# A macaron hybrid block on one Trainium2 core: hidden tiles turned by DMA are joined three weight products after they are parted, and the two newest units of down column 3 come after the seven-product block

## The chip, the cores and the metric

The kernel runs on one core of a Trainium2 chip. The metric is the device time of one execution in microseconds (us). Before the change its median over three runs was 1768.29 us (1766.9 to 1770.48). The engines are written as in the profile: PE is the matrix engine (PEld its weight loads), DVE the vector engine, ACT the scalar engine, SP the engine whose queue issues almost all DMAs.

## The reference

One layer: a half-step SwiGLU FFN, a mixer of two head groups, a second half-step FFN, a final norm. All in float32, 256 tokens, width 2048, FFN width 5632.

```python
def swiglu_ffn(x, w_gate, w_up, w_down):
    return (jax.nn.silu(x @ w_gate) * (x @ w_up)) @ w_down
...
    x = x + FFN_RESIDUAL_SCALE * swiglu_ffn(rms_norm(x, ffn1_norm[l]),
                                            ffn1_w_gate[l], ffn1_w_up[l], ffn1_w_down[l])
    z = rms_norm(x, mix_norm[l]) @ w_in[l]
...
    x = x + y @ w_out[l]
    x = x + FFN_RESIDUAL_SCALE * swiglu_ffn(rms_norm(x, ffn2_norm[l]),
                                            ffn2_w_gate[l], ffn2_w_up[l], ffn2_w_down[l])
return rms_norm(x, final_norm)
```

The change touches the two FFNs, and two small buffers of the norms.

## The kernel before, in words

**Weights.** Every weight comes as a unit of 512 rows by 512 columns (1 MB, tile `raw`). A unit is split into a high part (two ACT casts, `hi`) and the rest (one DVE subtraction, `lo`), and each matrix product is the sum of three matmuls: high by high, high by low, low by high (`parts_of`, line 173, and `multiply`, line 198). One call of `multiply` is one weight product: 12 matmuls of 512 columns for one token tile, 24 for two. There are three sets of `hi`/`lo` buffers in an FFN, three `raw` buffers, and two more (`kept`) that take the first two units of every seven-product block and, in the FFN, two of every five other units.

**FFN.** The FFN width is cut into 11 units of 512. Unit 0 is made first. Then stage s (0 to 4) makes two more units: a seven-product block for the gate (`seven`, line 343, called in line 738), one for up (line 739). A seven-product block is a 2x2 block product (2 token tiles by 2 column units, first two row units) with seven products of 12 matmuls in place of eight, with sums of the weights made by DVE in place (`raw` minus `raw`), and the other row units by the usual products of 24 matmuls: two of them per column unit in gate and up. Its loads are all emitted at its beginning. `done` hands out each of its four results as it is complete: in the up block that is `up` (line 730), which multiplies by the gate's silu and calls `turn_hidden` (line 423). After stages 0, 2 and 4 `down` (line 646) multiplies the finished units (three, four, four of them) by their rows of the down matrix and adds to the residual `xres`.

**Turning a tile.** Down needs the hidden tile with FFN columns on the partitions. `turn_hidden` parts a tile of 128x512 floats into two planes of 16-bit halves (ACT, tile `plane`), lets a DMA on SP's queue transpose it (line 431), joins the halves again (ACT, back into `plane`), splits it into high (ACT) and low (DVE) in `hidden[u]`, and where the tile is the newest of a down, copies it back once more (`turned`, ACT). There is one `plane` buffer, so the next tile can be parted only when the one before is joined and split. Each up block makes four tiles, unit 0 two: 44 tiles in all.

**Down.** Of its units, m and n are the two newest, the others are older. Column 0 and column 3 of the output are plain sums over units (`add_units`, line 660: one load, one split, one product of 24 matmuls per unit); columns 1 and 2 are one seven-product block in which m and n are the 2x2 block and the others the usual products. `block_sums` (line 679) makes the sums of the m and n tiles that the block needs. In stage 0 there is one other unit, in stages 2 and 4 two. The order of the calls stands in `plan` and `tail` (lines 693 to 707):

- stage 0: column 0 of others and n, column 3 of the other and n, column 0 of m, sums, column 3 of m, block;
- stage 2: column 0 of others and n, column 3 of others, column 0 of m, sums, column 3 of n and m, block (in FFN 1 with `prepare`, small vectors of the mixer, ahead of it);
- stage 4: column 0 of others and n, column 3 of others, column 0 of m, sums, block, column 3 of n and m.

**Order.** A tile scheduler puts the instructions of each engine in an order when the program is built; earlier code has precedence, but an instruction that is expected to be ready goes ahead of one that is not. Engines work their queue in that order. Only stretches with `Engine.pinned` keep the order of the code.

Nearly all rows of the profile name line 43, the helper that issues instructions; so they are read by tile names: `ps_g`, `ps_u`, `ps_d` are products of gate, up and down, `_a _c _e _d` the four banks of a seven-product block, `hi_.._p`/`lo_.._p` the split units of its seven products, `_x` those of its usual ones, `hs` the sums of hidden tiles, `u_g`, `z`, `s_g` the tiles that hold hidden tiles, `h` the turned tile's halves.

Of the kernel before, what the change touches and what calls it, by code (L numbers as in the profile page):

```python
# [10 lines left out]
F32 = mybir.dt.float32  # L11
F32R = mybir.dt.float32r
U16 = mybir.dt.uint16
# [4 lines left out]
P = 128  # L18
# [31 lines left out]
def hybrid_block(ctx: ExitStack, tc: tile.TileContext, a: dict, out: bass.AP):  # L50
# [35 lines left out]
    def f32(ap):  # L86
        return ap.bitcast(F32)
# [252 lines left out]
    def quad(tile):  # L340
        return tile.rearrange("p (j c) -> p j c", j=UK)
# [63 lines left out]
    def ffn(tag, norm, after, opening=False):  # L405
        with (
# [8 lines left out]
                return fp.tile([P, CW], dt, tag="keep", name=name, bufs=13)  # L415

            def plane():
                return fp.tile([P, CW], F32, tag="plane", name=f"plane{tag}", bufs=1)

            hidden = {}  # L420
            turned = {}

            def turn_hidden(u, t, h, again):

                if u not in hidden:
                    hidden[u] = big(f"h{tag}_{u}")
                pt = plane()
                mixed = "p (f b) -> p b f"
                flat = "p (b f) -> p b f"
                act.copy(pt.bitcast(U16).rearrange(flat, b=2), h.bitcast(U16).rearrange(mixed, b=2))  # L430
                nc.sync.dma_start(
                    h.bitcast(U16).rearrange("p (r c) -> p r c", c=P), pt.bitcast(U16), transpose=True
                )
                act.copy(pt.bitcast(U16).rearrange(mixed, b=2), h.bitcast(U16).rearrange(flat, b=2))
                pt = pt.rearrange("p (j c) -> p j c", j=UK)
                hi = hidden[u][:, :, t * P : (t + 1) * P]
                lo = hidden[u][:, :, S + t * P : S + (t + 1) * P]
                act.copy(hi, pt)
                dve.tensor_tensor(lo, pt, f32(hi), op=ALU.subtract)
                if again:  # L440
                    act.copy(quad(h), pt)
                    turned[u, t] = quad(h)

            units, vs, sf, ready = [], {}, {}, []

# [198 lines left out]
            turn_of["hold"] = False  # L644

            def down(last):
                us = sorted(hidden)
                others, (m, n) = us[:-2], us[-2:]
                end = last and tag == 2

                def update(c, t, *parts):
                    xr = xres[:, t, c * CW : (c + 1) * CW]
                    for p in parts:
                        dve.scalar_tensor_tensor(xr, p, 0.5, xr, op0=ALU.mult, op1=ALU.add)
                    if last:
                        after(c, t)

                side = {c: [bank(f"ps_d{tag}_{m}_{c}_{t}") for t in range(NT)] for c in (0, 3)}

                def add_units(c, units):  # L660
                    blks = [
                        (u, unit(wd[u * UK * P : (u + 1) * UK * P, c * CW : (c + 1) * CW], f"d{tag}_{m}_{c}_{u}"))
                        for u in units
                    ]
                    groups = [[0], [1]] if end and units == [n, m] else [[0, 1]]
# [12 lines left out]

                def block_sums():
                    seven_of(  # L680
                        sh, hidden[m], hidden[n],
                        {(t, i): turned[u, t] for t in range(NT) for i, u in ((0, m), (1, n))},
                        quad(keep(f"hspare{tag}_{m}")),
                        [[quad(keep(f"hs{tag}_{m}_{i}_{z}", F32R)) for z in range(2)] for i in range(4)],
                    )()

                def add(t, b, ps, tiles):
                    got[t, b] = [ps] + tiles
                    if (0, b) in got and (1, b) in got:
                        for i in range(NT):  # L690
                            update(2 - b, i, *got[i, b])

                plan = [(0, [u]) for u in others + [n]] + [(3, [u]) for u in others]
                if len(others) == 1:
                    plan.append((3, [n]))
                plan.append((0, [m]))
                tail = [(3, [n, m])] if end else [(3, [u]) for u in (n, m) if (3, [u]) not in plan]
                for step in plan:
                    add_units(*step)
                block_sums()  # L700
                if not last:
                    for step in tail:
                        add_units(*step)
                if tag == 1 and m == 5:
                    prepare()
                seven(wd, (m, n), (2 * CW, CW), sh, [(u, hidden[u]) for u in others], f"d{tag}_{m}", keep, add)
                if last:
                    for step in tail:
                        add_units(*step)
                hidden.clear()  # L710
                turned.clear()

            for s in range(5):
# [26 lines left out]
                if s % 2 == 0:  # L740
                    down(s == 4)
            extra.clear()


    def small(name):
# [337 lines left out]
```

## Time and profile before

| | |
|---|---|
| median of 3 runs | 1768.29 us |
| the profiled execution | 1769.3 us |
| its span, first to last instruction | 1767.5 us |
| mean granted PE clock | 0.991 |
| PE, weight loads, DVE, ACT busy | 1721.6, 1419.8, 1486.8, 1137.2 us |
| HBM read | 339.82 MB, 193 GB/s over the span |
| hidden tiles turned (casts of `h` out of `plane`) | 44 |
| transposing DMA, issue to landing | 3.0 to 7.8 us |

Busy time is a union of spans; matmuls overlap, and 20182 instructions are shared out over the engines. A row of the windows gives a stretch, its length, and busy time with the number of instructions of each engine in it; the granted clock is in parts of full speed.

### The profile page before, as it was taken

Reading aid. Unit: us, or ns where it says so; the run is one execution under the profiler, and the core shown is the slowest. Engines: PE = TensorE matmul, PEld = TensorE weight load, DVE = VectorE, ACT = ScalarE, POOL = GpSimd, SP = SyncE. Lnnn points to the kernel's source line nnn. Section 1 sums busy time; section 2 is a strip of 40 time slices with the busy share of each in tenths; the row PEclk is TensorE's granted clock in tenths of the full one; section 3 lists DMA queues with packets and bytes.
Section 4 is the critical chain, followed back from the end, with each engine's and each line's share of the span. In section 5 each row is a group of like instructions: output and inputs, shape, how many; then the busy total and the mean of one; then the engine's idle time right before and its main releaser. Section 6 shows DMA issues by size and latency. Waiting matters only on the chain. (4 is left out here: it accounts for less than half of the span.)

```text
span 1767.5 us, 20182 instructions
## 1 busy us (share of the span) xinstructions
PE 1721.6 (97%) x7859; PEld 1419.8 (80%) x7859; DVE 1486.8 (84%) x1233; ACT 1137.2 (64%) x1433; POOL 6.9 (0%) x32
## 2 busy tenths in 40 slices
PE   8999899999999999999999999999899999999998
PEld 6887687887887887888888888777687888887876
DVE  7996988878898979687987669978889978989776
ACT  6866466775567676665665456675567665677764
POOL 1000000000000000000000000000000000000000
PEclk9999899999999999999999999999899999999999
DMA  8666456684566683555556564694566665566843
GB/s 297 193 223 206 166 176 201 219 269 137 190 237 199 216 276 131 198 174 195 184 191 212 195 213 131 208 275 136 190 213 197 226 221 191 190 202 216 265 150 120
DMA packets 220384, 354.76 MB, mean 201 GB/s; under 512 B 52100, under 2 KB 54528, under 8 KB 220160
## 3 DMA queue, kind: packets, MB, share of 16 engines
q1 hardware_dynamic: 219824, 352.36, 61.3%
q8 instruction: 61, 1.00, 0.2%
q10 hardware_dynamic: 144, 1.05, 0.1%
q14 instruction: 35, 0.29, 0.0%
q0 software_dynamic: 320, 0.07, 0.0%
HBM read 339.82 MB, written 2.10 MB: 193 GB/s over the span
## 5 line engine op out<-in xcount | busy, mean ns | idle before, releaser
L43 PE MATMUL ps_d<-hi_d,h 128*128 128x512 f32 x704 | 172.5, 396 | 7.9 <-DVE h L43 3.8
L43 DVE TENSOR_TENSOR lo_g_p<-raw_g,hi_g_p 128x2048 fp32r<-128x2048 f32 x66 | 150.8, 2288 | 35.0 <-ACT hi_g_p L43 34.5
L43 ACT CAST hi_u_p<-raw_u 128x1024 fp32r<-128x1024 f32 x140 | 141.7, 1048 | 56.0 <-DVE raw_u L43 29.7
L43 DVE TENSOR_TENSOR lo_u_p<-raw_u,hi_u_p 128x2048 fp32r<-128x2048 f32 x70 | 159.3, 2286 | 12.8 <-ACT hi_u_p L43 12.4
L43 PEld LDWEIGHTS ps_d<-hi_d,h 128*128 128x128 f32 x704 | 133.2, 190 | 39.9 <-DVE h L43 6.3
L43 ACT CAST hi_g_p<-raw_g 128x1024 fp32r<-128x1024 f32 x132 | 134.0, 1046 | 45.7 <-DVE raw_g L43 25.6
L43 PE MATMUL ps_in<-xT_nm,hi_in 128*128 128x512 f32 x640 | 153.4, 391 | 0.0
L43 DVE TENSOR_TENSOR lo_d<-raw_d,hi_d 128x2048 fp32r<-128x2048 f32 x44 | 100.8, 2290 | 54.6 <-ACT hi_d L43 54.5
L43 PEld LDWEIGHTS ps_in<-xT_nm,hi_in 128*128 128x128 f32 x640 | 117.3, 188 | 23.2 <-ACT tha L43 0.4
L43 ACT CAST hi_d_p<-raw_d 128x1024 fp32r<-128x1024 f32 x84 | 84.8, 1046 | 74.5 <-DVE raw_d L43 43.1
L43 ACT CAST hi_in<-raw_in 128x1024 fp32r<-128x1024 f32 x80 | 80.0, 1046 | 63.4 <-PE ps_in L43 43.3
L43 DVE TENSOR_TENSOR lo_in<-raw_in,hi_in 128x2048 fp32r<-128x2048 f32 x40 | 91.3, 2285 | 34.5 <-ACT hi_in L43 31.8
L43 DVE TENSOR_TENSOR lo_d_p<-raw_d,hi_d_p 128x2048 fp32r<-128x2048 f32 x42 | 95.2, 2287 | 16.7 <-ACT hi_d_p L43 16.7
L43 ACT CAST hi_u_x<-raw_u 128x1024 fp32r<-128x1024 f32 x80 | 80.4, 1047 | 43.9 <-DMA raw_u<-in_ffn_w_up_dram 17.3
L43 DVE TENSOR_TENSOR raw_u<-raw_u,raw_u 128x2048 f32<-128x2048 f32 x40 | 91.6, 2291 | 12.0 <-DMA raw_u<-in_ffn_w_up_dram 11.3
L43 ACT CAST hi_d<-raw_d 128x1024 fp32r<-128x1024 f32 x88 | 89.6, 1045 | 17.5 <-PE ps_d L43 4.6
L43 DVE TENSOR_TENSOR lo_g_x<-raw_g,hi_g_x 128x2048 fp32r<-128x2048 f32 x40 | 91.5, 2286 | 5.2 <-ACT hi_g_x L43 4.9
L43 DVE TENSOR_TENSOR lo_u_x<-raw_u,hi_u_x 128x2048 fp32r<-128x2048 f32 x40 | 91.4, 2285 | 0.7 <-ACT hi_u_x L43 0.7
L43 ACT CAST hi_g_x<-raw_g 128x1024 fp32r<-128x1024 f32 x80 | 81.3, 1045 | 14.2 <-PE ps_g_c L43 7.0
L43 PE MATMUL ps_d<-lo_d,h 128*128 128x512 f32 x352 | 87.5, 389 | 0.0
L43 DVE TENSOR_TENSOR raw_g<-raw_g,raw_g 128x2048 f32<-128x2048 f32 x37 | 84.6, 2287 | 0.9 <-DMA raw_g<-in_ffn_w_gate_dram 0.5
L43 PEld LDWEIGHTS ps_in<-xT_nm,lo_in 128*128 128x128 f32 x640 | 82.1, 191 | 3.1
(387 smaller groups left out, 3677.6 us busy)
## 6 DMA issues: line engine op xcount, KB each, us to landing
raw_d<-in_ffn_w_down_dram SPq DMA_DIRECT2D x88, 1024.0 KB, 5.3
raw_u<-in_ffn_w_up_dram SPq DMA_DIRECT2D x87, 1024.0 KB, 5.3
raw_g<-in_ffn_w_gate_dram SPq DMA_DIRECT2D x86, 1024.0 KB, 5.4
raw_in<-in_w_in_dram SPq DMA_DIRECT2D x40, 1024.0 KB, 5.1
raw_o<-in_w_out_dram SPq DMA_DIRECT2D x16, 1024.0 KB, 5.1
xres<-in_x_dram SPq DMA_DIRECT2D x4, 512.0 KB, 8.0
raw_u<-in_ffn_w_up_dram SPq DMA_DIRECT2D x2, 512.0 KB, 9.4
raw_g_first<-in_ffn_w_gate_dram SPq DMA_DIRECT2D x1, 1024.0 KB, 12.3
```

Source lines behind the costliest of these rows:

```text
L43: ins = getattr(self.engine, name)(*args, **kwargs)
```

## The change

`multiply` calls the functions in a new list `after_product` after every weight product. `turn_hidden` is split into `part` (first ACT copy, DMA) and `join` (the rest). A tile that is handed in waits in `tiles`; at most two are `moving`, each with a plane of its own (`plane` has two buffers). `onward`, called after every product, joins a tile once three products have been emitted since it was parted. The two planes cost 2 KB more per partition; `diag` and `bc` of the norms go from two buffers to one. `down` takes all units that are there or on the way, and has one order for all stages: column 0 of others and n, column 3 of others, column 0 of m, sums, block, column 3 of n and m. So in stage 0 column 3 of n moves from before column 0 of m, and column 3 of m from before the block, to after the block; in stage 2 both move from before the block to after it; in stage 4 nothing moves.

```diff
+    after_product = []
+
     def multiply(targets, blk, apart=False, middle=None):
...
                 pe.matmul(ps, st[j][0], blk[j][1], start=False, stop=end and j == UK - 1, **more)
+        for fn in after_product:
+            fn()
...
-                dg = work.tile([P, P], F32, tag="diag", name=f"diag_{self.name}_{t}")
+                dg = work.tile([P, P], F32, tag="diag", name=f"diag_{self.name}_{t}", bufs=1)
...
-            self.bc = work.tile([P, S], F32, tag="bc", name=f"bc_{self.name}")
+            self.bc = work.tile([P, S], F32, tag="bc", name=f"bc_{self.name}", bufs=1)
...
-                return fp.tile([P, CW], F32, tag="plane", name=f"plane{tag}", bufs=1)
+                return fp.tile([P, CW], F32, tag="plane", name=f"plane{tag}", bufs=2)
...
-            def turn_hidden(u, t, h, again):
-
+            mixed, flat = "p (f b) -> p b f", "p (b f) -> p b f"
+            tiles, moving = deque(), deque()
+
+            def part(u, t, h, again):
+                two = plane()
+                act.copy(two.bitcast(U16).rearrange(flat, b=2), h.bitcast(U16).rearrange(mixed, b=2))
+                nc.sync.dma_start(
+                    h.bitcast(U16).rearrange("p (r c) -> p r c", c=P), two.bitcast(U16), transpose=True
+                )
+                return two
+
+            def join(two, u, t, h, again):
                 if u not in hidden:
                     hidden[u] = big(f"h{tag}_{u}")
-                pt = plane()
...
+                act.copy(two.bitcast(U16).rearrange(mixed, b=2), h.bitcast(U16).rearrange(flat, b=2))
+                two = quad(two)
                 hi = hidden[u][:, :, t * P : (t + 1) * P]
                 lo = hidden[u][:, :, S + t * P : S + (t + 1) * P]
-                act.copy(hi, pt)
-                dve.tensor_tensor(lo, pt, f32(hi), op=ALU.subtract)
+                act.copy(hi, two)
+                dve.tensor_tensor(lo, two, f32(hi), op=ALU.subtract)
                 if again:
-                    act.copy(quad(h), pt)
+                    act.copy(quad(h), two)
                     turned[u, t] = quad(h)
+
+            def turn_hidden(*tile):
+                tiles.append(tile)
+                begin_some()
+
+            def begin_some():
+                while tiles and len(moving) < 2:
+                    tile = tiles.popleft()
+                    moving.append([0, tile, part(*tile)])
+
+            def onward():
+
+                for entry in moving:
+                    entry[0] += 1
+                while moving and moving[0][0] >= 3:
+                    _, tile, two = moving.popleft()
+                    join(two, *tile)
+                begin_some()
...
-                us = sorted(hidden)
+                us = sorted(set(hidden) | {tile[0] for tile in on_the_way()})
...
-                plan = [(0, [u]) for u in others + [n]] + [(3, [u]) for u in others]
-                if len(others) == 1:
-                    plan.append((3, [n]))
-                plan.append((0, [m]))
-                tail = [(3, [n, m])] if end else [(3, [u]) for u in (n, m) if (3, [u]) not in plan]
-                for step in plan:
-                    add_units(*step)
+                for c, u in [(0, u) for u in others + [n]] + [(3, u) for u in others] + [(0, m)]:
+                    add_units(c, [u])
                 block_sums()
-                if not last:
-                    for step in tail:
-                        add_units(*step)
                 if tag == 1 and m == 5:
                     prepare()
                 seven(wd, (m, n), (2 * CW, CW), sh, [(u, hidden[u]) for u in others], f"d{tag}_{m}", keep, add)
-                if last:
-                    for step in tail:
-                        add_units(*step)
+                for units in [[n, m]] if end else [[n], [m]]:
+                    add_units(3, units)
```

More of the change, by code (lines that the diff above doesn't have):

```diff
@@ L425, in turn_hidden @@
+            def join(two, u, t, h, again):
                 if u not in hidden:
                     hidden[u] = big(f"h{tag}_{u}")
-                pt = plane()
[L428 to L433, printed above, removed]
@@ L434, in turn_hidden @@
-                act.copy(pt.bitcast(U16).rearrange(mixed, b=2), h.bitcast(U16).rearrange(flat, b=2))
-                pt = pt.rearrange("p (j c) -> p j c", j=UK)
+                act.copy(two.bitcast(U16).rearrange(mixed, b=2), h.bitcast(U16).rearrange(flat, b=2))
+                two = quad(two)
                 hi = hidden[u][:, :, t * P : (t + 1) * P]
                 lo = hidden[u][:, :, S + t * P : S + (t + 1) * P]
-                act.copy(hi, pt)
-                dve.tensor_tensor(lo, pt, f32(hi), op=ALU.subtract)
+                act.copy(hi, two)
@@ L444, in ffn, with on_the_way @@
+            def onward():
[5 more added lines that the diff above has]
+                begin_some()
+            def on_the_way():
+                return [*tiles, *(entry[1] for entry in moving)]
+            after_product.append(onward)
             units, vs, sf, ready = [], {}, {}, []
@@ L664, in add_units @@
                     ]
+                    assert not {tile[0] for tile in on_the_way()} & set(units)
                     groups = [[0], [1]] if end and units == [n, m] else [[0, 1]]
@@ L742, in ffn @@
             extra.clear()
+            after_product.clear()
     def small(name):
```

## The prediction

> **What bounds the kernel now.** I start with the page's first part.
>
> ```profile
> span 1767.5 us, 20182 instructions
> PE 1721.6 (97%) x7859; PEld 1419.8 (80%) x7859; DVE 1486.8 (84%) x1233; ACT 1137.2 (64%) x1433; POOL 6.9 (0%) x32
> ```
>
> PE is busy for 97% of the span and its work does not change (the same matmuls, in another order). So a gain can only come out of stretches in which PE runs late, and I need those by stage: the windows view of PE, cut at the first product of each block.
>
> ```profile
> core 0: us, PE busy (x), PEclk, DMA share, GB/s
> 140.48:207.43 66.95, 64.72 (x280) 1.00 0.54 171
> 207.43:257.03 49.60, 43.81 (x179) 0.90 0.58 198
> 257.03:297.83 40.80, 40.80 (x182) 1.00 0.66 215
> 297.83:341.02 43.19, 42.13 (x182) 1.00 0.67 211
> 381.82:469.44 87.62, 85.45 (x376) 1.00 0.63 201
> 635.43:710.62 75.19, 74.31 (x325) 1.00 0.57 186
> 1174.48:1241.32 66.84, 64.21 (x279) 1.00 0.56 171
> 1241.32:1291.45 50.13, 43.71 (x180) 0.90 0.57 196
> 1416.30:1501.27 84.97, 84.66 (x374) 1.00 0.63 205
> 1582.95:1626.15 43.20, 42.14 (x182) 1.00 0.67 211
> 1666.95:1747.69 80.74, 76.88 (x326) 0.96 0.53 163
> ```
>
> The measure is the third row: an up block of 180 matmuls (seven products of 12, four of 24) in 40.80 us without a gap, 0.2267 us each. (The x counts also take matmuls that overlap an edge; I count from the code.) What each stretch loses against that:
>
> - Down of stage 0 is 6 units of 24 plus 132 in its block, 276 matmuls, 62.6 us: the first row loses 4.4, its twin in FFN 2 (1174.48) 4.3.
> - The gate block behind it should take 40.8: it loses 8.8 and 9.3 (207.43 and 1241.32).
> - The gate blocks of stages 2 and 4, which follow an up block directly, lose 2.4 each in both FFNs (first and last of the four: 297.83 and 1582.95), 9.6 in all.
> - Stage 2's down with the gate behind it is 192 + 180 matmuls, 84.3: it loses 3.3 (381.82) and 0.7 (1416.30).
> - Stage 4's down up to its block's end is 144 + 180, 73.5: it loses 1.7 in FFN 1 and 7.2 in FFN 2.
>
> Together about 49 us, 2.8% of the span: the ceiling of this change. Two causes make up most of it. The first is read from the chain of waits around the gap in the gate block:
>
> ```profile
> 1237.68 2.30 DVE lo_d_p L43
> ...
> 1239.99 6.89 DMA raw_g<-in_ffn_w_gate_dram
> ...
> 1246.98 2.30 DVE raw_g L43
> ...
> 1249.36 1.05 ACT hi_g_p L43
> ```
>
> A `kept` buffer comes free when DVE has split a unit of the down block that ends (`lo_d_p`, done at 1239.98). Only then is the gate's second unit loaded; its difference and its cast follow, and PE, which ended the down block at about 1241, gets its second product at 1250.4. There is nothing between the two blocks for PE to do meanwhile.
>
> The second cause is the turning. The tile view of `plane` says what ACT waits for, and the ACT timeline how:
>
> ```profile
>   DMA u_g<-plane: 20.6, 14
> ...
>   DMA z<-plane: 12.9, 9
>   DMA s_g<-plane: 11.0, 8
> ...
> DMA to landing us min/median/max: 3.0/3.6/7.8
> ```
>
> ```profile
> 1685.32 1.05 ACT L43 COPY plane<-s_g 128x1024 uint16<-128x1024 uint16 x1 [1.98 <-DVE h L43]
> 1686.27 2.00 ACT L43 CAST hi_d<-raw_d 128x1024 fp32r<-128x1024 f32 x2
> ...
> 1692.81 1.35 ACT L43 COPY plane<-s_g 128x1024 uint16<-128x1024 uint16 x1 [3.07 <-DMA s_g<-plane]
> ```
>
> ACT stands 44.5 us at the second copy of a tile (20.6 + 12.9 + 11.0). Some other casts are put between the two copies, too few. And with one plane the four tiles go in single file, which the chain of waits shows at the last down, beside the DVE timeline:
>
> ```profile
> 1675.85 1.04 ACT plane L43
> ```
>
> ```profile
> 1663.52 0.69 DVE L43 TENSOR_TENSOR z<-ps_u_a,z 128x512 f32<-128x512 f32 x1 [0.47 <-PE ps_u_a L43]
> ```
>
> Tile `z` was there at 1664.2 and was parted at 1675.85, 11.6 us later; the last tile is joined after 1692.81, when PE already wants it. That is most of the 7.2.
>
> **The change part by part.**
>
> *Two planes, joins after three products (all FFN stages).* No instruction is added: per tile the same ACT copies, one DMA, one DVE subtraction. A tile no longer waits for its forerunner's join, so in the last down `z` is parted at about 1664.3, and even with the longest landing (7.8) and the join (1.35 by the row of 1692.81, and some 1.3 for cast and subtraction) it is there by about 1675; `s_g` similarly before 1685. PE needs m's tiles as the sixth unit there, 5 x 5.44 us after 1666.95, at 1694. So the stall at the last down goes; I leave it the 1.7 of its twin: gain 5.5. In the four gate blocks ACT's stops are what delays the casts; the same DMAs now start earlier and overlap, and joins yield to the casts of three products. I do not expect all stops to go, since nothing ties the ACT queue to the count of products; of 2.4 I leave 1.0: gain 5.6, bounded by 0 and 9.6. On SP the transposes stand where they stood, ahead of the next block's loads, but are issued sooner, so what is queued behind them is not later.
>
> *Column 3 of n and m after the block, stage 0.* Two units, 48 matmuls, 10.9 us, now lie between the down block and the gate block. The gate's second unit is issued at the same point as before, about 1.5 us ahead of the down block's end, and needs 6.89 + 2.30 + 1.05 = 10.2; its product is wanted 10.9 + 2.7 after the end. The gap is covered with 5 us to spare, if the two units themselves are loaded in time: in stage 0 they are the fifth and sixth unit outside blocks, so they use `raw` buffers, which the block's middle frees some 8 us before its end, against 5.3 for a load. What is late next is the down block: it loses two units of cover ahead of it, and DVE is its tightest engine.
>
> ```profile
> 174.91:206.23 31.32, 29.97 (x130) 23.87 (x129) 28.76 (x21) 18.43 (x23) 0.00 (x0) 1.00 0.43 141
> 668.55:710.62 42.07, 41.34 (x181) 33.49 (x180) 38.75 (x27) 27.89 (x37) 0.00 (x0) 1.00 0.49 169
> ```
>
> Columns: stretch, length, then PE, weight loads, DVE, ACT, GpSimd. In stage 0's block DVE (third) is busy 28.76 of 31.32 us, and the sums (eight operations, one every 0.6 us by the starts of 171.37 and 171.97 below) partly fall inside. The second row is the block of FFN 1's last down, which already has the order that all downs get: DVE 38.75 of 42.07, and yet its whole down loses 1.7. The four units ahead of stage 0's block offer DVE 21.8 us of PE time for four splits of 2.29, two joins, the sums and the block's first split and difference, 9.2 + 1.2 + 4.9 + 4.6 = 19.9, provided that the last tile is joined early, which the two planes bring. It is tight, so I leave 2.5 where the last down has 1.7. Of 13.2 and 13.6 (down and gate) that gains 10.7 + 11.1 = 21.8; bounds: 26.8 if nothing is left, and a loss of about 9 per down if the block starts cold (below).
>
> *The same in stage 2.* Its down has two other units, so the gate block had no gap to cover. The wait for turned tiles goes, the cover ahead of the block shrinks, `prepare` now stands directly ahead of it. The two units after the block are the third and fourth of their five and take `kept` buffers, so the gate's first two units wait for their splits; those are made about a product ahead, a load is 5.3 us, and the gate's second product comes 13.6 us after the block. I leave 2 in both FFNs: 1.3 gained, 1.3 lost, 0 (bounds +4 and two gaps of 9).
>
> *One `diag`, one `bc`.* `bc` is made twice, far apart: nothing. The second `diag` must now wait for the first one's matmuls, so PE waits for one more DVE operation and its signal, in two norms:
>
> ```profile
> L43 DVE TENSOR_SCALAR diag_nm<-ident,r_nm x2: 282/284/286, 727.7 to 727.9; 128x128 f32<-128x128 f32 x2
> ```
>
> 0.3 plus signals, 0.6 each, 1.2 lost (bounds 0 and 3).
>
> Sum: 5.5 + 5.6 + 21.8 + 0 - 1.2 = 31.7 us. Off the profiled execution's 1769.3 that is 1737.6; the median shown is 1.0 lower, so **1737 us**.
>
> [...]
>
> **The rivals.**
>
> *ACT's order does not change (chance 0.2).* The count of products only moves the join in the code; the scheduler may put it into ACT's queue as soon as it thinks the DMA landed, as it did at 1692.81. For it: nothing but readiness orders ACT, and ACT has 36% idle time to fill. Against: the second plane starts transposes earlier in any case. Then the gates gain nothing and the last down half, while the cover between blocks stays: 21.8 + 2.7 - 1.2 = 23 less, and with half of the stage 0 downs' own losses kept, 18 to 23 less: about 1748, from 1744 to 1762 where stage 2 also loses something.
>
> *Gain and loss cancel (0.05):* 1765 to 1772.
>
> *The down block starts cold (0.15), slower.* One mechanism at one place: in the four downs of stages 0 and 2 DVE comes to the block's second product late, because sums, column 0's updates (which wait for its last product) and the first difference all queue behind one another. Then PE waits there as it did in the gate block: split 2.29, difference 2.30, cast 1.05, and matmuls at half clock, 9 us by the rows of 207.43 and 1241.32; the next product, also made by a difference and a cast, adds 3.4. Four times 12.4 is 50 lost against 31.7 gained: 1786. It turns slower from 8 us per down. Against: in the DVE timeline of stage 0 the block's first difference stands ahead of column 0's second update and of sums (`s_g`), and the last down of FFN 1 works in this order.
>
> ```profile
> 169.17 2.29 DVE L43 TENSOR_TENSOR raw_d<-raw_d,raw_d 128x2048 f32<-128x2048 f32 x1
> 171.37 0.68 DVE L43 SCALAR_TENSOR_TENSOR xres<-ps_d,xres 128x512 f32<-128x512 f32 x1
> 171.97 0.68 DVE L43 TENSOR_TENSOR s_g<-hspare,s_g 128x512 f32<-128x512 f32 x1
> ```
>
> **How the numbers follow.** Forecast 0.60, with 1722 to 1744 as its own range: the low end is the ceiling of 49 less a few us, the high end the forecast with stage 2 at its bad end. With the rivals, faster by over 0.2% is 0.60 + 0.20 = 0.80, within 0.2% (3.5 us, about what a measurement here tells from no change) 0.05, slower 0.15. The range 1722 to 1767 leaves out the slower rival and some 0.05 elsewhere.
>
> **What would show it.** Right: the stretch from down's first product to the up block in stage 0 shrinks from 116.6 and 117.0 to about 106; no half clock near 215 and 1250; ACT's waits for `plane` DMAs well below 44.5; the four gate blocks near 41.8; the last down near 75. Wrong: a wait of PE inside `ps_d_c` or `ps_d_a` of stages 0 or 2 for a `hi_d_p` behind DVE, a gate block of stage 2 or 3 waiting for `raw_g`, or ACT still at the second copy for 40 us, which would refute my reading of the planes.

## The result and the profile after

The changed kernel takes 1748.92 us (median of four runs, 1748.26 to 1749.68) against 1769.33 (four runs, 1766.9 to 1770.48): a ratio of 0.9887, interval 0.9869 to 0.9904. It is 20.4 us faster; 31.7 had been forecast. The profiled execution took 1749.3 us, against 1769.3 before, so the traces differ by 20.0 us and can be compared block by block.

The page's first part, after: PE has the same 7859 matmuls and is now busy for 98%, in 11.5 us less PE time (1721.6 before), because less of it runs at a low clock (mean granted clock 0.997, 0.991 before).

```profile
span 1747.3 us, 20171 instructions
PE 1710.1 (98%) x7859; PEld 1417.5 (81%) x7859; DVE 1486.1 (85%) x1233; ACT 1137.4 (65%) x1433; POOL 6.9 (0%) x32
```

The windows view of PE, cut as before at the first product of each block (stretch, length, PE busy and its matmuls, granted clock, DMA share, GB/s):

```profile
core 0: us, PE busy (x), PEclk, DMA share, GB/s
140.73:206.31 65.58, 63.16 (x278) 1.00 0.60 198
206.31:247.11 40.80, 40.80 (x182) 1.00 0.60 206
287.91:330.95 43.04, 41.48 (x182) 1.00 0.65 208
371.75:456.56 84.81, 84.81 (x375) 1.00 0.64 205
538.16:582.25 44.09, 41.77 (x181) 1.00 0.63 203
1163.56:1228.24 64.68, 63.21 (x278) 1.00 0.62 198
1228.24:1271.45 43.21, 41.55 (x182) 1.00 0.56 191
1312.53:1356.45 43.92, 41.73 (x182) 1.00 0.63 204
1563.69:1608.56 44.87, 41.77 (x182) 1.00 0.62 203
1649.36:1727.72 78.36, 75.37 (x325) 0.98 0.51 168
```

Each stretch is compared with its matmuls at 0.2267 us, 24 to a unit, as the prediction did. The gate block behind stage 0's down (206.31) runs without a gap in FFN 1 and loses 2.4 in FFN 2 (1228.24), where 8.8 and 9.3 were lost, and the clock there is 1.00, not 0.90. But the four gate blocks that follow an up block (287.91, 538.16, 1312.53, 1563.69) got **longer**: 43.0 to 44.9 us.

The table gives the same for the kernels that follow, from the first and last product of each block: us lost against 0.2267 per matmul, both FFNs together. "Other" is the gate block that opens each FFN and FFN 2's first up block. Stage 4's downs hold 0.8 in every row for products of the norm behind FFN 1, which run among their last matmuls. (Cut exactly at the gate's first product, the gaps behind stage 0's downs were 10.2 and 10.7 us before; the prediction's rows had 1.4 of each on the down's side, with the same sum of 26.8.)

| kernel | stage 0: down and the gate behind | four gate blocks behind up | stage 2 downs | stage 4 downs | other | sum | profiled execution |
|---|---|---|---|---|---|---|---|
| before | 26.8 | 9.8 | 3.9 | 10.7 | 3.8 | 55.0 | 1769.3 |
| after | 7.5 | 12.7 | 1.0 | 8.2 | 5.6 | 35.0 | 1749.3 |
| order alone | 15.1 | 10.0 | 6.6 | 11.0 | 4.0 | 46.6 | 1761.5 |
| turning alone | 12.1 | 12.1 | 0.5 | 10.5 | 6.4 | 41.4 | 1756.1 |
| after, joined at once | 13.4 | 21.8 | 1.3 | 7.2 | 7.4 | 51.1 | 1765.3 |
| after, one plane | 16.5 | 9.9 | 3.3 | 8.6 | 5.3 | 43.7 | 1759.7 |
| after, five products | 7.7 | 10.7 | 1.5 | 4.3 | 2.1 | 26.2 | 1741.6 |
| after, eight products | 8.1 | 2.9 | 0.5 | 3.1 | 1.8 | 16.4 | 1731.1 |
| eight, old order | 13.3 | 4.2 | 0.5 | 2.7 | 2.0 | 22.6 | 1737.9 |
| after, twelve products | 10.6 | 2.3 | 0.5 | 2.8 | 0.5 | 16.6 | 1731.8 |

Before and after differ by 20.0 in the sums and in the executions, so no time is left unexplained by block (the mixer changed by 0.3).

What ACT waits for, in the tile view of `plane` (us, times), after. The four DMA rows add up to 28.5 us; before, three such rows made 44.5.

```profile
  DMA u_g<-plane: 13.9, 8
  DMA s_g<-plane: 10.4, 6
  DMA z<-plane: 2.2, 5
  DMA sg<-plane: 2.0, 1
...
DMA to landing us min/median/max: 3.0/3.8/8.3
```

Why the gate blocks grew is in the timeline around the start of FFN 2's stage 4 gate at 1563.69 (start, length, then the instruction and, in brackets, the engine's idle time before it and what ended it):

```profile
1554.29 1.24 SPq L433 DMA_TRANSPOSE u_g<-plane  x1
...
1562.05 1.35 ACT L43 COPY plane<-u_g 128x1024 uint16<-128x1024 uint16 x1 [3.46 <-DMA u_g<-plane]
1563.43 0.62 ACT L43 CAST h<-plane 128x512 fp32r<-128x512 f32 x1
1563.96 1.04 ACT L43 COPY plane<-z 128x1024 uint16<-128x1024 uint16 x1
1564.08 0.69 DVE L43 TENSOR_TENSOR h<-plane,h 128x512 fp32r<-128x512 f32 x1 [2.48 <-ACT h L43]
1564.69 2.29 DVE L43 TENSOR_TENSOR raw_g<-raw_g,raw_g 128x2048 f32<-128x2048 f32 x1
...
1567.01 1.99 ACT L43 CAST hi_g_p<-raw_g 128x1024 fp32r<-128x1024 f32 x2
...
1568.11 2.13 PE L43 MATMUL ps_g_c<-hi_g_p,xs 128*128 128x512 f32 x8 [1.54 <-ACT hi_g_p L43]
1569.39 1.36 ACT L43 COPY plane<-z 128x1024 uint16<-128x1024 uint16 x1
1570.62 1.04 ACT L43 COPY plane<-s_g 128x1024 uint16<-128x1024 uint16 x1
1572.64 0.74 PE L43 MATMUL ps_g_c<-lo_g_p,xs 128*128 128x512 f32 x2 [0.81 <-DVE lo_g_p L43]
```

Read it from the top. The transpose of `u_g` is issued at 1554.29 and lands at about 1562.0, 7.7 us later. ACT is free for the join at 1558.6, 5.4 us after it began to part this tile (1553.21), and the data is not there: it stands 3.46 us. In the code three products lie between the two, which take PE 13.6 us (two of 24 matmuls, one of 12), so the count of products does not say how long ACT takes from one to the other. DVE has the join's subtraction at the head of its queue and stands 2.48 us; behind that subtraction stands the gate block's difference of `raw_g`, which starts 1.0 us after the block and whose cast `hi_g_p` (1567.01) PE then waits for, 1.54 us. Then `z` is parted and joined and `s_g` parted, all inside the first 10 us of the gate block.

### The profile page after: what moved, and what is told of

It reads as the page before. It is cut to its first block, busy times and chain, and to the rows that moved or that the text cites. A ratio compares the mean times of both kernels' runs of the same rounds, so it can differ in the third digit from the quotient of the medians.

```text
span 1747.3 us, 20171 instructions
## 1 busy us (share of the span) xinstructions
PE 1710.1 (98%) x7859; PEld 1417.5 (81%) x7859; DVE 1486.1 (85%) x1233; ACT 1137.4 (65%) x1433; POOL 6.9 (0%) x32
## 5 line engine op out<-in xcount | busy, mean ns | idle before, releaser
L43 PE MATMUL ps_d<-hi_d,h 128*128 128x512 f32 x704 | 167.2, 389 | 0.0
L43 DVE TENSOR_TENSOR lo_d<-raw_d,hi_d 128x2048 fp32r<-128x2048 f32 x44 | 100.7, 2289 | 21.1 <-ACT hi_d L43 19.8
## 6 DMA issues: line engine op xcount, KB each, us to landing
raw_g_first<-in_ffn_w_gate_dram SPq DMA_DIRECT2D x1, 1024.0 KB, 12.1
```

The costliest lines, as they stand in the source:

```text
L43: ins = getattr(self.engine, name)(*args, **kwargs)
```

## The experiments

**My theory** after the result: the cover behind stage 0's down works, and three products are too short a delay, because a join called for too early stops ACT and DVE ahead of a gate block. (The cover holds; that three products are a delay does not, as told behind the run with twelve products.) **Rivals:** the place of the join in the code does not reach ACT's queue (the prediction's rival); the order of down alone, or the turning alone, does it all; the transposes' landing is what counts; DVE, busier than ACT (85% and 65% of the span), should lose the join's subtraction.

**Order alone.** The kernel before, with only the new order of down (one plane, joins in place).

```diff
-                plan = [(0, [u]) for u in others + [n]] + [(3, [u]) for u in others]
...
+                for c, u in [(0, u) for u in others + [n]] + [(3, u) for u in others] + [(0, m)]:
+                    add_units(c, [u])
                 block_sums()
...
+                for units in [[n, m]] if end else [[n], [m]]:
+                    add_units(3, units)
```

> The order of down alone, with one plane and joins in place as before. Theory A (the order of down brings nearly all of the 20 us, the turning next to nothing): 1769 - 18 = about 1751; the gate blocks of stage 0 lose under 2 us each, from 8.8 and 9.3. Theory B (the order needs the second plane: with one, the last tile is joined about 25 us after down's first product, and in this order column 0 of m wants it 16 us after): the gaps in the gate blocks go too, but PE waits 6 to 9 us for `h` ahead of column 0 of m in each stage 0, with half clock behind it, so about 1765, and a wait of PE on `h` of over 12 us in all.

Measured: 1758.61 us, ratio 0.9947 (0.9928 to 0.9965). The windows of stage 0's two downs, and what the tile view of `plane` says of those who wait for turned tiles:

```profile
140.31:210.90 70.59, 66.19 (x278) 0.95 0.57 184
...
1170.26:1238.23 67.97, 65.18 (x278) 0.97 0.59 185
```

```profile
  PE ps_d L43: 14.4, 9
```

The gate gap closes (0 and 1.7 lost, 10.2 and 10.7 before), but down loses 8.0 and 5.4 at a clock of 0.95 and 0.97: PE itself waits 14.4 us for `h`, 7.6 before. Of the 19.2 us that the gaps give, the downs take back 7.5 (5.9 to 13.4), because with one plane the last tile is late for the units that now come earlier. Stage 2's downs lose 2.7 more.

**Turning alone.** The changed kernel with the old order of down (the plan of four steps put back).

```diff
-                for c, u in [(0, u) for u in others + [n]] + [(3, u) for u in others] + [(0, m)]:
-                    add_units(c, [u])
+                plan = [(0, [u]) for u in others + [n]] + [(3, [u]) for u in others]
...
+                if not last:
+                    for step in tail:
+                        add_units(*step)
```

> The turning alone: two planes, joins after three products, one `diag` and one `bc`, with the order of down before. Theory A: the waits for turned tiles in the downs go (1.5 to 2.5 each, 5 or 6 in the last), the four gate blocks stay at 2.4 to 4 us lost, the gaps of 8.8 and 9.3 stay: 1769 - 5 = about 1764, between 1760 and 1769. Theory B: also about 1764; it says only that e1 and e2 do not add up to the whole change (e1 4 + e2 5 against 20).

Measured: 1754.03 us, ratio 0.9921 (0.9897 to 0.9944). The gate blocks behind stage 0's downs, in the windows view:

```profile
203.86:248.16 44.30, 41.86 (x181) 1.00 0.58 204
...
1235.72:1280.14 44.42, 41.85 (x181) 1.00 0.59 201
```

This missed what I had thought of the gap: with nothing between down and gate, it is 3.5 and 3.6 us, not 10, and at full clock. So the missing cover was not the gap's only cause: it closes to 0 and 1.7 by the order alone, and to 3.5 and 3.6 when tiles are joined earlier, without a unit put in between. In the times the two parts are worth 9.1 and 13.7 us, and together 20.4, nearly their sum. By block they overlap: in stage 0 they gain 11.7 and 14.7, together 19.3, and the order alone loses in stage 2 what the turning gives back.

**Joined at once.** The changed kernel, with the join called right behind the parting.

```diff
             def turn_hidden(*tile):
-                tiles.append(tile)
-                begin_some()
+                join(part(*tile), *tile)
```

> The changed kernel, but each tile is joined right where it is parted in the code, with two planes. If the count of products is only a place in the code and readiness puts the join into ACT's queue anyway: within 3 us of 1749. If the three products do keep ACT free: the gate blocks lose 2 us more each and downs 1 more, about 1760.

Measured: 1763.04 us, ratio 0.9977 (0.9963 to 0.9991), 14 us behind the changed kernel in the medians, 16 by the ratios. The first of its four gate blocks, and ACT's wait:

```profile
292.12:339.61 47.49, 43.65 (x181) 0.96 0.61 188
```

```profile
  ACT plane L43: 41.5, 27
```

So where the code calls for the join does reach the queues. ACT waits 41.5 us, nearly as long as before, and the four gate blocks lose 21.8 us, more than with one plane. In all four, by ACT's timeline, the join of `z` now stands between the two halves of a cast that PE needs for the block's second product (1582.41 and 1586.77 in the block from 1580.54, where the changed kernel makes both in a row), and the next join waits another 2.3 us.

**Five products.** If three are too few, five should help. Units that are about to be used need their tiles joined, so they ask for it.

```diff
-                while moving and moving[0][0] >= 3:
+                while moving and moving[0][0] >= 5:
...
+            def need(units):
+                while {tile[0] for tile in on_the_way()} & set(units):
+                    _, tile, two = moving.popleft()
+                    join(two, *tile)
+                    begin_some()
...
                 def add_units(c, units):
+                    need(units)
```

> The changed kernel with joins after five products (a tile that a down needs sooner is joined ahead of that). If the gate blocks lose because the join, with its wait for a DMA of up to 8 us, stands in ACT's and DVE's queue ahead of the block's first difference, a later place helps: the four gate blocks at 1 to 2 us lost each in place of 2.2 to 4, about 1743. If the place in the code does not reach the queues: 1749 within 3.

Measured: 1743.15 us, ratio 0.9866 (0.9845 to 0.9888). Faster, but the interval overlaps that of the changed kernel, and the gate blocks gain only 2.0. The timeline around the same gate block, which now begins at 1560.26:

```profile
1557.43 1.36 ACT L43 COPY plane<-u_g 128x1024 uint16<-128x1024 uint16 x1 [2.27 <-DMA u_g<-plane]
...
1559.47 0.69 DVE L43 TENSOR_TENSOR h<-plane,h 128x512 fp32r<-128x512 f32 x1 [1.30 <-ACT h L43]
1560.09 2.28 DVE L43 TENSOR_TENSOR raw_g<-raw_g,raw_g 128x2048 f32<-128x2048 f32 x1
```

DVE's wait at the join has halved (2.48 to 1.30), and the difference behind it starts 0.2 us ahead of the block instead of 1.0 behind. But the count did not do that. Up to there ACT and DVE work in the same order as with three products, in all four gate blocks, and ACT again comes to the join 5.4 us after it began to part the tile. The transpose landed earlier, 6.6 us after its issue against 7.7.

**Eight products.** The same with a longer delay:

```diff
-                while moving and moving[0][0] >= 5:
+                while moving and moving[0][0] >= 8:
```

> As e4, with eight products in place of five. Theory A (bunching: two planes bring the parting and joining of the last tiles into the first 10 us of the next gate block, where ACT and DVE have no slack; every product of delay moves a join out of it): the four gate blocks lose 8 us or less together, against 12.7 with three and 10.7 with five, and the whole is 1 to 3 us below e4's ratio of 0.9866. Theory B (a later join keeps its plane longer, the third and fourth tile are parted later, as with one plane): gate blocks back at 10 or more, stage 0's downs wait for `h` again, ratio 0.987 to 0.990.

Measured: 1733.09 us (1731.14 to 1737.76), ratio 0.9824 (0.9803 to 0.9846): it beats the kernel before and the changed one. The first and the last of the four gate blocks behind up in the windows view:

```profile
287.51:329.11 41.60, 41.49 (x182) 1.00 0.65 215
...
1552.32:1594.09 41.77, 41.48 (x182) 1.00 0.66 214
```

and the timeline of ACT and DVE around the last of them:

```profile
1547.73 0.69 DVE L43 TENSOR_TENSOR h<-plane,h 128x512 fp32r<-128x512 f32 x1
1548.33 2.29 DVE L43 TENSOR_TENSOR raw_g<-raw_g,raw_g 128x2048 f32<-128x2048 f32 x1
...
1549.51 1.36 ACT L43 COPY plane<-u_g 128x1024 uint16<-128x1024 uint16 x1 [2.09 <-DMA u_g<-plane]
...
1551.43 2.00 ACT L43 CAST hi_g_p<-raw_g 128x1024 fp32r<-128x1024 f32 x2
1551.56 0.69 DVE L43 TENSOR_TENSOR h<-plane,h 128x512 fp32r<-128x512 f32 x1 [0.33 <-ACT h L43]
1552.16 2.29 DVE L43 TENSOR_TENSOR raw_g<-raw_g,raw_g 128x2048 f32<-128x2048 f32 x1
```

ACT still stands 2.09 us at the join of the second `u_g` tile, nearly as long as with five. What has changed is the order: the difference for `hi_g_p` (1548.33) now stands ahead of that join's subtraction (1551.56) in DVE's queue, and starts 4.0 us ahead of the block's first product (1552.32) and not 1.0 behind it; its cast starts ahead of the block too, and `z` is parted behind that cast. The loss of the four blocks falls from 12.7 to 2.9 us, and ACT's waits for `plane` DMAs (8.4 + 2.9 + 2.5 by the tile view) to 13.8.

**Twelve products.** Is later better still?

```diff
-                while moving and moving[0][0] >= 8:
+                while moving and moving[0][0] >= 12:
```

> As e5, with twelve products in place of eight. Bunching says the gain levels off once the joins lie behind the gate block's first products: the four gate blocks stay near 3 us together, ratio 0.982 to 0.984. Against it a plane is kept longer, so the third and fourth tile are parted later; if that tells, the stage 0 downs lose 2 us more each (joins forced right ahead of their use), ratio 0.985.

Measured: 1731.78 us (1724.41 to 1734.12), ratio 0.9792 (0.9763 to 0.9821): not told apart from eight. The gates lose 2.3; FFN 2's down of stage 0 loses 5.1 (1.9 with eight), which takes it back.

**What the count of products moves.** The traces of these runs answer it. The first column is the median, over the 44 tiles, of the time from the end of a tile's parting to the point where ACT is free for its join; the second is ACT's waits for `plane` DMAs in the whole run; the third is where the gate block's first difference starts on DVE, against the block's first product, in the four gate blocks behind up.

| kernel | ACT: parted to join (us) | ACT waits (us) | first difference (us) | loss of the four |
|---|---|---|---|---|
| before | 3.3 | 44.5 | -2.2 to -1.9 | 9.8 |
| after, joined at once | 3.8 | 41.5 | -0.5 to 0.8 | 21.8 |
| after | 4.3 | 28.5 | -0.8 to 1.0 | 12.7 |
| after, five products | 4.3 | 26.9 | -1.0 to 0.3 | 10.7 |
| after, eight products | 4.8 | 13.8 | -4.0 | 2.9 |
| after, twelve products | 4.7 | 20.2 | -4.0 | 2.3 |

The count hardly moves the join on ACT, and ACT's wait is not what the gate blocks pay for: it is 20.2 us with twelve products and the blocks lose 2.3. They pay for the lateness of the difference. In the 16 gate blocks of the changed kernel, of the turning alone, of five products and of the run without squares (below), where DVE works in one order, the loss is the start of the difference plus 3.0 to 3.1 us, each time, from a start of -1.0 (2.0 lost) to 1.0 (4.1 lost). (With the joins at once it is 1.9 to 3.6 more, for the joins of `z` and of the tile after it.) In the code the join of the second `u_g` tile stands inside the up block with three products, right behind the gate block's first product and just ahead of its first difference with five, and behind two differences with eight. With eight it goes behind the first difference in DVE's queue too, and that is where the loss falls from 10.7 to 2.9.

**Eight, with the old order of down.** Does the order still matter once joins are late? The kernel with eight products, and the edit of the turning alone:

```diff
-                for c, u in [(0, u) for u in others + [n]] + [(3, u) for u in others] + [(0, m)]:
-                    add_units(c, [u])
+                plan = [(0, [u]) for u in others + [n]] + [(3, [u]) for u in others]
...
```

> As e5, with the order of down as before. If the gate gap of stage 0 was mostly lateness of DVE (which the late last tile brought), it stays small without units in between: about 3.5 each as in e2, and the whole is 6 to 8 us above e5, ratio 0.986. If the units between the blocks are what closes it, 9 each, 18 us above e5, ratio 0.992.

Measured: 1737.62 us, ratio 0.9831 (0.9817 to 0.9846). I had expected less gain. The interval overlaps both that of eight and that of twelve; the traces put stage 0 at 13.3 us lost against 8.1, with the gate blocks behind down at

```profile
203.80:248.17 44.37, 41.82 (x181) 1.00 0.58 203
...
1224.20:1268.38 44.18, 41.84 (x181) 1.00 0.58 201
```

So the order of down is worth about 5 us by the profile, and by the times something between nothing and that.

**One plane, joins late.** The changed kernel with one plane and one tile on its way, joins after three products (or as soon as a unit needs them).

```diff
-                return fp.tile([P, CW], F32, tag="plane", name=f"plane{tag}", bufs=2)
+                return fp.tile([P, CW], F32, tag="plane", name=f"plane{tag}", bufs=1)
...
-                while tiles and len(moving) < 2:
+                while tiles and len(moving) < 1:
```

> The changed kernel with one plane: joins after three products, one tile on the way at a time, joined ahead of its use where a down needs it sooner. If the second plane is what brings the last tile early: PE waits for `h` in the stage 0 downs as in e1 (8.0 and 5.4 lost), ratio 0.993 to 0.996. If it is the place of the join in the code that matters and the plane hardly does: within 3 us of the change, 0.988 to 0.990.

Measured: 1756.33 us, ratio 0.9944 (0.9928 to 0.9959). Stage 0's downs lose no less than in the order alone (8.3 and 7.0; 8.0 and 5.4 there):

```profile
142.03:212.88 70.85, 66.37 (x278) 0.95 0.56 183
1171.30:1240.83 69.53, 65.26 (x277) 0.98 0.60 186
```

The second plane is what brings the last tile early; the delay without it does not.

**Transposes from ACT's queue.** If the landing counts, and the landing is long because SP's queue is full of loads, ACT's own queue should shorten it. Two kernels, with five and with eight products:

```diff
-                nc.sync.dma_start(
+                nc.scalar.dma_start(
                     h.bitcast(U16).rearrange("p (r c) -> p r c", c=P), two.bitcast(U16), transpose=True
```

> As e4, with the transposing DMAs issued from ACT's queue in place of SP's. If landing (up to 8 us) is long because the transpose stands behind 1 MB loads that SP issued just before: landing falls to 3 to 4 us at most, ACT's wait for planes from 27 to under 15, ratio about 0.984. If it is the shared DMA engines, landing stays at 3 to 7 us, and ACT pays the issue (1.24 us on SP in the trace) 44 times, 55 us of its idle time: the gate blocks lose 1 to 2 us more each, ratio about 0.990.

> As e5, with the transposes on ACT's queue, which changed nothing clear at five products. The same as e5 within 2 us if it is only a reshuffling; 3 us less if the last down's 0.1 (against 1.4 to 2.0) is kept and nothing else moves.

Measured: 1741.79 us, ratio 0.9865 (0.9851 to 0.9880), against 0.9866 from SP's queue; with eight, 1741.99 us, 0.9858 (0.9829 to 0.9887), against 0.9824 (0.9803 to 0.9846). No gain. In the tile view, with five:

```profile
DMA to landing us min/median/max: 3.0/4.5/8.1
```

The landing is no shorter (3.0/4.1/7.0 from SP, same five products). The queue that issues is not what makes it long. With five products ACT's waits for `plane` DMAs did fall, from 26.9 to 9.1 us, as had been expected of a shorter landing, and the four gate blocks still lose 11.1 (10.7 from SP's queue): once more ACT's wait is not their price.

**The join's subtraction on GpSimd**, in the kernel with five products, to take work from DVE:

```diff
-                dve.tensor_tensor(lo, two, f32(hi), op=ALU.subtract)
+                nc.gpsimd.tensor_tensor(lo, two, f32(hi), op=ALU.subtract)
```

> As e4, with the low part of each turned tile made by GpSimd in place of DVE. If the gate blocks lose because DVE stands at `h`, waiting for ACT's cast, ahead of the block's first difference (1.8 us at 1306 to 1308 in e4's trace): the four blocks lose 1 us less each, ratio about 0.984. If ACT's own wait is what counts, they stay at 10.7. Against it: a GpSimd operation is likely slower than DVE's 0.69, and a down's product waits for it; then PE waits on `h` in downs and the ratio is above 0.987.

Measured: 1755.92 us, ratio 0.9942 (0.9925 to 0.9959), 13 us worse than with DVE. The row of the operation (minimum, median, maximum in ns):

```profile
L446 POOL TENSOR_TENSOR h<-plane,h x44: 1282/1725/5111, 70.9 to 1678.6; 128x512 fp32r<-128x512 f32 x44
```

It takes 1.73 us where DVE takes 0.69. The gates do not gain (12.0 lost), and the downs of all stages lose 26.1 us together (10.9 stage 0, 7.0 stage 2, 8.1 stage 4) against 13.4 with DVE (stage 0's with the gate behind it). Both the join and DVE's other work are longer: of the 45 operations of 128x2048 on weights that DVE ran beside one of these, 19 took 2.7 to 3.4 us, and none of its 510 took over 2.3 in the kernel with five products. What each costs was not separated.

**Without the final norm's squares of column 0**, work left out to see whether they hold up the last down. The changed kernel:

```diff
+    dve.memset(fss, 0.0)
...
-        act.activation(junk, xr, AF.Square, accum_out=part)
+        if c:
...
+            act.activation(junk, xr, AF.Square, accum_out=part)
```

> The changed kernel without the final norm's squares of column 0 (left out: the output's norm misses a quarter of its sum), which ACT works off at the start of the last down's block, ahead of the copy of its second bank. If they are what holds PE for 3 us there and halves the clock: the last down loses 1 to 1.5 us in place of 4.9, and the whole is 3 to 4 us below the change, ratio about 0.986. If the block there is late for DVE's differences alone: 4 or more still lost, 0.988 to 0.989.

Measured: 1749.24 us, ratio 0.9893 (0.9863 to 0.9924): the same as the changed kernel. In the last down the loss does fall, from 4.9 to 1.9 us, and the wait at `ps_d_c` from 3.0 to 1.8; but the down of FFN 1's stage 0, which the edit does not touch, lost 6.8 instead of 3.0. A gain of 3 us in one block is real in the trace and does not reach the total.

## Why the prediction was right in sign and short in size

- **Stage 0, predicted 21.8: right.** Measured 19.3 (26.8 to 7.5). From down's first product to the up block it takes 247.11 - 140.73 = 106.4 us and 1271.45 - 1163.56 = 107.9, where about 106 was said. The downs lose 3.0 and 2.1, where 2.5 was left. But its reason was incomplete: the prediction made the missing cover the cause of the gap, and the turning alone brings the gap to 3.5 us.
- **Four gate blocks, predicted a gain of 5.6: the step that failed.** Measured a loss of 2.9. The step said that "the same DMAs now start earlier and overlap, and joins yield to the casts of three products". The DMAs do start earlier, and the join does not yield. Before, the second `u_g` tile was parted 2.7 us ahead of the last of these blocks, and on DVE both differences stood ahead of its join. With two planes it is parted 10.5 us ahead, so in all four blocks its join and the wait for its landing (1.7 to 3.5 us on ACT) stand ahead of the gate's first difference: the earlier start that was counted as the gain is what made the loss. With one plane and the same three products the blocks lose 9.9, as before the change. And the three products do not hold the join back, since ACT comes to it 4.3 us (median) after parting. What stood behind the join on DVE did not go ahead of it: by the timeline of after, the two units of the last block's first difference had landed by 1554.6 and the split of the first ended at 1560.4, yet DVE stood idle for 2.48 us up to 1564.08 and made the difference only behind the join's subtraction. The step's lower bound was 0; joins at once make it a loss of 12.0. With eight products, where the difference goes first, the blocks gain 6.9, inside the 9.6 that was the ceiling.
- **Last down, predicted 5.5: right in kind, 2.4 measured** (7.3 to 4.9). Late tiles are gone, and another wait stands there, on ACT: the copy of the bank. By ACT's timeline of after:

```profile
1688.80 0.57 ACT L43 COPY s_d<-ps_d_a 128x512 f32<-128x512 f32 x1
...
1691.77 0.58 ACT L43 COPY s_d<-ps_d_c 128x512 f32<-128x512 f32 x1
```

  PE waited 3.0 us for the second, behind two casts of the next product. Without the squares it waits 1.8.
- **Stage 2, predicted 0: 2.9 gained.** I left 2 in each FFN for the lost cover; 0.5 was lost. The prepared units and their `kept` buffers were in time.
- **One `diag`, one `bc`, predicted -1.2: -0.3**, the change of the mixer. The part of the 1.2 that was put down to signals was an estimate that no row shows. In after, at the first of the two norms, DVE waits 0.27 us for PE ahead of the second `diag`, and PE's weight loads then 0.35 for DVE; at the second norm the weight loads wait 0.2.
- **Not in the sum:** the first gate block of stage 0 lost 0.5 and 1.9 more, FFN 2's up block 0.7 less. The first two are gone with five and with eight products, where these blocks lose 0.2 each.

Together: 19.3 - 2.9 + 2.4 + 0.1 (FFN 1's last down) + 2.9 - 0.3 - 2.4 + 0.7 = 19.8 of the 20.0 measured. That the total lies within the stated range owes something to luck: the gates came out 8.5 us worse than forecast and the last down 3.1, and stage 2's 2.9 were not forecast at all.

Of the rivals, "ACT's order does not change" comes closer than its chance of 0.2: it said about 1748, with nothing gained by the gates, half by the last down and the cover kept, and that is nearly what was measured (1748.92; -2.9, 2.4 of 5.5, 19.3 of 21.8). Its reason is right in that the count hardly moves the join on ACT (3.8 to 4.8 us from parting, at once to twelve products), and wrong in that the place in the code counts for nothing: 14 us hang on it with the joins at once, and eight products put the gate's difference first. "The block starts cold" is there in small with the second plane and short of the 12.4 us of its price: in FFN 1's stage 0, PE waits 2.4 us for `lo_d_p`; the worst down, that of the run without squares, loses 6.8. What comes nearest is another thing: with one plane stage 0's downs lose 8.0 and 5.4, 8.3 and 7.0 us at clocks of 0.95 to 0.98, but there PE waits at the units for a turned tile, not at the block's second product for DVE. The second plane takes that away.

FFN 1's stage 0 down lost 3.8 us more when only the end of the kernel was edited. The trace shows how: PE waited 2.93 us for `lo_d_p` in place of 2.42, and behind it the clock was at 0.50 for 6.8 us, where it had stayed at 1.00. Open is why the losses of these downs move with edits elsewhere, between 0.7 and 6.8 us in kernels with two planes; so one block of one trace does not prove an effect that small.

## What to carry to other kernels

In these runs a result that arrived by DMA and had to pass through ACT and DVE stopped what stood behind it (ACT for 3.46 us and DVE for 2.48 at the changed kernel's last gate block), and the price showed in the next block, not where the wait is written. So call for it behind the instructions that the next block waits for. Counting products does not give it time: here ACT came to the join 4 to 5 us after parting whatever the count, and landings took up to 8.3. What paid was the place in DVE's queue, behind the next block's first difference, and that is read from DVE's timeline. A second buffer and a later join need each other: the buffer without the delay cost the gate blocks 12.0 us, and the delay without the buffer left the last tile late. Where two edits close the same gap, their gains there are not added: predict each alone, then ask what is left for the other.

## What the runs showed of the hardware

A transposing DMA of 256 KB lands 3.0 to 8.3 us after its issue in the changed kernel, median 3.8, and not sooner from ACT's queue than from SP's (medians 4.5 and 4.1 with five products).

DVE's operations of 128x2048, 2.29 us else, took 2.7 to 3.4 us in 19 of the 45 that ran beside a subtraction on GpSimd.

Before the change the clock fell behind PE's wait of 6.16 us in FFN 2's gate block behind stage 0's down (stretch, length, then PE, weight loads, DVE, ACT, GpSimd, and the clock):

```profile
1243.00:1257.00 14.00, 7.74 (x21) 5.74 (x22) 12.53 (x8) 3.60 (x5) 0.00 (x0) 0.63 0.37 127
```

By the windows view it was 0.50 from 1250.45, where the wait ends, to 1255.90, and 0.50 from 213 to 220 at the same place in FFN 1.

In after the clock fell behind a shorter wait: PE waited from 1689.4 to 1692.4, and the windows view gives the clock of the stretches from there on.

```profile
1689.40:1692.40 3.00, 0.01 (x1) 1.00 0.28 28
1692.40:1696.00 3.60, 3.60 (x11) 0.70 0.70 268
1696.00:1700.00 4.00, 4.00 (x16) 0.85 0.62 205
```

3.0 us of idle PE cost another 3.6 + 4.0 us at 0.70 and 0.85 of the clock: 27 matmuls where 34 fit, 1.5 us. The wait's length is by the profile, whose matmul ends are modelled. The length of one gap does not decide it here: behind a wait of 1.80 us, at the second product of FFN 1's stage 0 block with eight products, the clock was halved as well,

```profile
169.00:172.40 3.40, 3.40 (x10) 0.50 0.24 66
```

and behind one of 2.42 us at the same product of the changed kernel (from 167.2) it stayed at 1.00. What decides between them is open. In the last down, without the squares, the wait is 1.8 us, and the block loses 3.0 us less.
